# Mixture-of-experts weights in 8192-byte pieces, and expert slots scattered through memory, in a fused transformer layer

## The chip, the cores and the metric

The kernel runs on one core of a Trainium2 chip. The metric is the device time of one execution in microseconds (us). The profile is that of one execution by the hardware profiler; its engines are PE (TensorE matmul), PEld (TensorE weight load), DVE (VectorE), ACT (ScalarE), POOL (GpSimd) and SP (SyncE, which here only issues DMAs).

## The reference

One trunk layer of a generator over 512 latent tokens (and 256 context tokens) of width 2048. A first sub-layer mixes tokens with three recurrent heads groups; the change does not touch it. The second is a hierarchical mixture of experts over the 512 normalised tokens:

```python
grp = jnp.argmax(pg, -1)                      # 1 of 4 groups
top_p, top_i = lax.top_k(softmax(le), 2)      # 2 of its 8 experts
# every expert e (32 of them), on the tokens sent to it:
y = (silu(x @ w_gate[e]) * (x @ w_up[e])) @ w_down[e]   # 2048 -> 512 -> 2048
f = sum of a token's two y, weighted; out = rmsnorm(x + gt2 * f)
```

All is float32. The weights of the experts are 32 x 3 x 4 MB.

## The kernel before

The first 1890 us of the program (input projection, three recurrent mixers, output projection) stay as they are. Then come three stages.

**Routing** (`route_setup`, `route_tile`, `route_slots`). `route_slots` makes on DVE, for the tokens as 4 tiles of 128 rows, the one-hot rows `o1`, `o2` of the two chosen experts, the token's rank `pos` within each expert, and on POOL the weights `wm`. Each expert has 64 slots; `over` and `njob` count blocks of tokens beyond 64. `moe_over` is a hardware loop of `njob` rounds for those; all engines meet in front of it and behind it, and with no such block its body is skipped.

**Weights** (`moe_weights`, `load`, `slot`). SP streams all expert weights through a ring of 10 slots of 1 MB. `moe_weights` lists the chunks in the order of use: 8 gate/up chunks of an expert, 4 down chunks (half the columns of a pair of experts), and so on; `gf` is the last norm's gain. Four slots are there early (`more_slots(r0, NR)`), six after the output projection. A chunk of gate and up is 256 rows of each matrix, read by two DMAs of 512 KB, in which a partition gets two rows that lie together (4096 bytes); a down chunk is one DMA of 1 MB in pieces of 4096 bytes. Each `load()` waits until PE has used what was in the slot.

**Experts** (`phase_moe`). For each group of 4 experts `gather` makes a one-hot matrix `G` on DVE (`moe_hot`) and, for each of 8 slices of 256 rows, four products of 256 columns each with a high (`hh`, ACT) and a low part (`hl`, DVE, every fourth on POOL); the result `xg` is 256 slots wide. `gate_up(e)` multiplies `xg` with the ring: in each of 8 steps j there are 2 rows-of-128 times 2 halves `c` of columns, each product 64 slots by 512 columns (256 of gate beside 256 of up), the two halves in the two column halves of the array; a float32 product is two MATMUL instructions in the trace. It then loads the next chunk and calls the other work that is listed for step j. `turn` transposes, `down` multiplies with the down chunks, `combine` brings the slots back to the tokens with a one-hot `GT` and adds to `x1`. `slots(pr)` makes `GT` and the slots' weights `W` for a pair of experts, in three pieces: one-hot rows `Gp` on DVE, four PE transposes and an ACT copy, four PE products with `wm` and two DVE copies. PE's order in this stage is that of the code (`keep_in_program_order`).

Of the kernel before, what the change touches and what calls it, by code (L numbers as in the profile page):

```python
# [11 lines left out]
F32 = mybir.dt.float32  # L12
F32R = mybir.dt.float32r
BF = mybir.dt.bfloat16
# [38 lines left out]
class Kern:  # L53
# [1439 lines left out]
    def route_setup(self, op):  # L1493
# [27 lines left out]
        self.iota1k = rp.tile([P, 32], F32, name="iota1k")  # L1521
        nc.vector.tensor_scalar(self.iota1k, self.iota[:, :32], 1000.0, None, op0=OP.add)
        self.thr = rp.tile([P, 7], F32, name="thr")
        nc.vector.tensor_scalar(self.thr, self.iota[:, 1:8], 64.0, None, op0=OP.mult)
# [39 lines left out]
    def route_slots(self, tp):  # L1564
# [8 lines left out]

        def first_max(vals, n, oh, mx):
            t_ = mk(f"t{n}", n)
            ix = mk("ix", 1)
# [4 lines left out]
            nc.vector.tensor_tensor(oh, self.iota[:, None, :n].to_broadcast([P, 4, n]), bc(ix, n), op=OP.is_equal)  # L1581

        gm, og = mk("gm", 1), mk("og", 4)
        first_max(lgr, 4, og, gm)
        eg = mk("eg", 4)
# [12 lines left out]
        m1, m2, o1, o2 = mk("m1", 1), mk("m2", 1), mk("o1", 32), mk("o2", 32)  # L1598
        first_max(me, 32, o1, m1)
# [3 lines left out]
        first_max(me2, 32, o2, m2)  # L1603
        A = mk("A", 32)
# [31 lines left out]
        nc.gpsimd.tensor_tensor(me, o2, bc(e12[:, :, 1:2], 32), op=OP.mult)  # L1636
        nc.gpsimd.tensor_tensor(self.wm, self.wm, me, op=OP.add)

    def moe_hot(self, dst, es):
# [37 lines left out]
    def load(self):  # L1677
        nc, I = self.nc, self.I
        ch = next(self.todo, None)
        if ch is None:  # L1680
            return
        if ch == "gf":
            self.gf = self.slot([P, D], True)
            nc.sync.dma_start(self.gf, I["g_final"].rearrange("(o c) -> o c", o=1).to_broadcast([P, D]))
            return
        e, c = ch
        if type(c) is int:
            w = self.slot([P, 2, 2, 512])
            for j, nm in enumerate(("moe_w_gate", "moe_w_up")):
                nc.sync.dma_start(w[:, j], I[nm][0, e, 2 * c * P:(2 * c + 2) * P].rearrange("(p k) c -> p k c", k=2))  # L1690
        else:
            h, f = c
            w = self.slot([P, 2, D // 2])
            nc.sync.dma_start(w, I["moe_w_down"][0, e, 2 * f * P:(2 * f + 2) * P, h * D // 2:(h + 1) * D // 2].rearrange("(f p) c -> p f c", p=P))
        self.wgt[ch] = w

    def phase_moe(self):
        nc, tc = self.nc, self.tc
        wgt, load, NE = self.wgt, self.load, self.ne
        with tc.tile_pool(name="mo", bufs=1) as mo, tc.tile_pool(name="ps5", bufs=1, space=PSUM) as ps:  # L1700
# [9 lines left out]
            def gather(q):  # L1710
# [6 lines left out]
                for k0 in range(0, KT, 2):  # L1717
                    x = self.xgp.tile([P, 2, 256], F32, name=f"xg{k0 // 2}")
                    xg[q].append(x)
                    p = ps.tile([P, 2, 256], F32, name="pc_", bufs=4)  # L1720
                    for k in range(2):
                        h = self.h2[:, :, k0 * P + k:(k0 + 2) * P:2]
                        hh = mo.tile([P, 4, P], F32R, name="hh", bufs=2)
                        hl = mo.tile([P, 4, P], F32R, name="hl", bufs=2)
                        nc.scalar.copy(hh, h)  # L1725
                        (nc.gpsimd if k and k0 % 4 == 0 else nc.vector).tensor_tensor(hl, h, hh.bitcast(F32), op=OP.subtract)  # L1726
                        for i, hx in enumerate((hh, hl)):
                            for t in range(4):
                                mm(p[:, k], hx[:, t], G[:, t].rearrange("p e s -> p (e s)"), start=(i == t == 0), stop=(i == 1 and t == 3))
                    nc.scalar.copy(x, p)  # L1730
                    yield

            def slots(pr):

                es = (2 * pr, 2 * pr + 1)
                GT = mo.tile([P, S], F32R, name="GT", bufs=2)
                W = mo.tile([P, 1], F32, name="Wsl", bufs=2)
                Gp = mo.tile([P, 4, 2, 64], F32, name="Gp", bufs=1)
                self.moe_hot(Gp, es)
                yield  # L1740
                p = ps.tile([P, 4, P], F32, name="ts", bufs=1)
                for t in range(4):
                    tr(p[:, t], Gp[:, t].rearrange("p e s -> p (e s)"), self.ident)
                nc.scalar.copy(GT, p.rearrange("p t c -> p (t c)"))
                yield
                pw = ps.tile([P, 2], F32, name="ts", bufs=1)
                for t in range(4):
                    mm(pw, Gp[:, t].rearrange("p e s -> p (e s)"), self.wm[:, t, es[0]:es[0] + 2], start=(t == 0), stop=(t == 3))
                for i in range(2):
                    nc.vector.tensor_copy(W[64 * i:64 * i + 64], pw[64 * i:64 * i + 64, i:i + 1])  # L1750
                gts[pr] = (GT, W)
                yield

            def gate_up(e, *work):
# [3 lines left out]
                for j in range(KT // 2):  # L1758
                    g = wgt[e, j]
                    for k in range(2):  # L1760
                        for c in range(2):
                            mm(p[64 * c:64 * c + 64], x[j][:, k, 64 * (e % 4):64 * (e % 4) + 64], g[:, :, k, 256 * c:256 * c + 256],
                               start=(j == k == 0), stop=(j == 7 and k == 1), tile_position=(0, 64 * c))
                    load()
# [51 lines left out]
            for pr in range(NE // 2):  # L1816
                a = 2 * pr
                sl = slots(pr)
                if pr == 0:
# [4 lines left out]
                else:  # L1824
                    two = () if pr % 2 else ((0, partial(next, gat)),) * 2 + ((4, partial(next, gat)),) * 2
                    gate_up(a, *two, (1, partial(turn, a - 1)), (2, combine), (5, combine))
# [21 lines left out]
    def fin(self, mo, t, col):  # L1848
# [5 lines left out]
        sf = self.sf[:, t]  # L1854
        sq = mo.tile([P, col[1]], BF, name="sq3", tag="Gp", bufs=1)
        nc.scalar.activation(sq, x[:, cs], AF.Square, accum_out=sf[:, b:b + 1])
# [186 lines left out]
    def tail(self, ctx):  # L2043
# [22 lines left out]
        with ExitStack() as s:  # L2066
# [4 lines left out]
            next(r)  # L2071
            fin()
            next(r, None)
        self.moe_over()
# [83 lines left out]
```

## Time and profile before

| what | us |
|---|---|
| three runs: lowest, median, highest | 2979.39, 2993.38, 2997.74 |
| the profiled execution, its own time | 2985.22 |
| its span in the trace | 2983.5 |

The span is from the first to the last instruction of the trace. In the sections below, a row of a timeline has start (us from the span's start), length (us), engine, line and operation, output <- inputs, shape and count, and in brackets the idle time before it and what ended it. Matmuls overlap, so the pace of PE is read from one start to the next, not from a length.

### The profile page before, as it was taken

To read this page: it belongs to the slowest core of one execution; us is meant where nothing else is said; L and a number is where in the kernel's file an instruction comes from. 1 tells how busy PE (TensorE), PEld (TensorE's weight loads), DVE (VectorE), ACT (ScalarE), POOL (GpSimd) and SP (SyncE) were. 2 spreads that over 40 slices of the span, in tenths; PEclk is the share of its full clock that TensorE was granted. 3 is DMA by queue.
4 is the path that set the end of the run, shared out by engine and by line. 5 is a ranking of instruction groups with operands and counts; after the bars stand their busy time and mean duration, and the time that the engine had idled before them with its cause. 6 is when DMAs were issued, how large, how long until landed. Compare 5 with 4: busy or idle time off the path is not lost. (4 is left out here: it accounts for less than half of the span.)

```text
span 2983.5 us, 50569 instructions
## 1 busy us (share of the span) xinstructions
PE 2730.6 (92%) x19229; PEld 1798.6 (60%) x19229; DVE 1563.5 (52%) x3165; ACT 839.5 (28%) x1632; POOL 751.2 (25%) x715
## 2 busy tenths in 40 slices
PE   5989999988999999988989898879999999999997
PEld 3477787778767766766766666744454444544433
DVE  4366566688477565565446656642343333433335
ACT  4132322345432223322222322332121221211212
POOL 2332222231344443343344434520000000000001
PEclk9999999998999999999979989989999999999999
DMA  8858787887744344444465321469999999999997
GB/s 303 294 171 242 225 253 231 246 251 224 194 108 117 96 121 101 106 116 104 104 212 181 110 87 43 135 237 409 408 409 409 408 409 408 407 409 407 409 408 290
DMA packets 530909, 730.80 MB, mean 245 GB/s; under 512 B 121233, under 2 KB 347839, under 8 KB 529507
## 3 DMA queue, kind: packets, MB, share of 16 engines
q1 hardware_dynamic: 366864, 640.77, 59.9%
q10 hardware_dynamic: 161927, 81.17, 10.7%
q0 software_dynamic: 1872, 5.57, 0.6%
q8 instruction: 155, 2.54, 0.4%
q14 instruction: 91, 0.75, 0.1%
HBM read 672.50 MB, written 54.93 MB: 244 GB/s over the span
## 5 line engine op out<-in xcount | busy, mean ns | idle before, releaser
L1705 PE MATMUL pgu<-ring,xg 128*64 128x512 f32 x2048 | 484.4, 600 | 1.9 <-DVE sil__20834 L1770 0.9
L319 POOL TENSOR_TENSOR wl<-wr,wh 128x512 fp32r<-128x512 f32 x191 | 263.3, 1379 | 691.0 <-ACT wh L318 600.5
L61 PE MATMUL pl<-hil,wh 128*128 128x512 f32 x928 | 404.0, 436 | 4.3 <-ACT hil L253 3.7
L61 PE MATMUL pl<-lol,wh 128*128 128x512 f32 x928 | 376.4, 406 | 0.1
L61 PE MATMUL pl<-hil,wl 128*128 128x512 f32 x928 | 372.0, 401 | 0.5 <-POOL wl L319 0.4
L318 ACT CAST wh<-wr 128x512 fp32r<-128x512 f32 x292 | 179.6, 619 | 576.9 <-PE pl L61 316.7
L1705 PEld LDWEIGHTS pgu<-ring,xg 128*64 128x64 f32 x2048 | 135.1, 136 | 239.5 <-issue 225.3
L1726 POOL TENSOR_TENSOR hl<-h,hh 128x512 fp32r<-128x512 f32 x32 | 41.8, 1306 | 823.6 <-ACT hh L1725 823.6
L1705 PE MATMUL py<-ring,hT 128*64 128x512 f32 x1024 | 235.2, 593 | 3.5 <-DMA ring<-in_moe_w_down_dram 3.5
L271 DVE SCALAR_TENSOR_TENSOR acc<-w,sil,acc 128x512 f32<-128x512 f32 x240 | 197.6, 851 | 59.5 <-DMA w<-in_w_ada_dram 58.2
L61 PEld LDWEIGHTS pl<-hil,wh 128*128 128x128 f32 x928 | 178.8, 193 | 60.4 <-issue 14.4
L61 PEld LDWEIGHTS pl<-hil,wl 128*128 128x128 f32 x928 | 178.9, 193 | 41.2 <-POOL wl L319 1.2
L61 PEld LDWEIGHTS pl<-lol,wh 128*128 128x128 f32 x928 | 179.5, 193 | 38.5 <-issue 6.7
L1705 PEld LDWEIGHTS py<-ring,hT 128*64 128x64 f32 x1024 | 76.2, 137 | 155.8 <-issue 139.4
L61 PE MATMUL pc<-hic,wl 128*128 128x256 f32 x496 | 146.1, 295 | 14.4 <-DVE wl L319 10.5
L61 PE MATMUL pc<-hic,wh 128*128 128x256 f32 x496 | 146.3, 296 | 4.8 <-ACT wh L318 2.8
L61 PE MATMUL pc<-loc,wh 128*128 128x256 f32 x496 | 145.7, 295 | 1.1 <-DVE loc L254 1.1
L1725 ACT CAST hh<-h 128x512 fp32r<-128x512 f32 x128 | 84.8, 664 | 165.9 <-PE pc__23508 L1705 9.0
L1726 DVE TENSOR_TENSOR hl<-h,hh 128x512 fp32r<-128x512 f32 x96 | 66.6, 694 | 119.0 <-ACT hh L1725 114.8
L791 DVE TENSOR_TENSOR ptm<-Tm,Lay 64x1 f32<-64x1 f32 (+2 forms) x270 | 109.1, 404 | 22.3 <-DMA Lay<-s_ad 15.9
L1796 DVE SCALAR_TENSOR_TENSOR yt<-py,Wsl,g 128x512 f32<-128x512 f32 x64 | 48.1, 751 | 133.3 <-PE py L1705 133.3
L1443 POOL TENSOR_TENSOR wol<-wo,woh 128x512 fp32r<-128x512 f32 x56 | 75.3, 1347 | 159.7 <-PE acc L61 97.8
(2215 smaller groups left out, 4960.1 us busy)
## 6 DMA issues: line engine op xcount, KB each, us to landing
ring<-in_moe_w_gate_dram SPq DMA_DIRECT2D x256, 512.0 KB
ring<-in_moe_w_up_dram SPq DMA_DIRECT2D x256, 512.0 KB
ring<-in_moe_w_down_dram SPq DMA_DIRECT2D x128, 1024.0 KB
wr<-in_w_in_dram ACTq DMA_DIRECT2D x288, 256.0 KB
w<-in_w_ada_dram SPq DMA_DIRECT2D x256, 256.0 KB
w<-in_w_ada_dram SPq DMA_DIRECT2D x64, 512.0 KB
wo<-in_w_out_dram SPq DMA_DIRECT2D x56, 256.0 KB
rv_xk<-d_xk SPq DMA_DIRECT2D x36, 256.0 KB
```

The costliest lines, as they stand in the source:

```text
L61: i = self.nc.tensor.matmul(*a, **k)
L271: nc.vector.scalar_tensor_tensor(acc, w, self.sil[:, k, 0:1], acc, op0=OP.mult, op1=OP.add)
L318: nc.scalar.copy(wh[:, :, :n], wr[:, :, :n])
L319: (nc.vector if q in self.wdve else nc.gpsimd).tensor_tensor(wl[:, :, :n], wr[:, :, :n], wh[:, :, :n].bitcast(F32), op=OP.subtract)
L791: nc.vector.tensor_tensor(pt_[:, :t, :t], Tm[:, :t, :t], Lay[:, :t, t].rearrange("q (o s) -> q o s", o=1).to_broadcast([64, t, t]), op=OP. ...
L1443: nc.gpsimd.tensor_tensor(wl, w, wh.bitcast(F32), op=OP.subtract)
L1705: pin(nc.tensor.matmul(*a, **k))
L1725: nc.scalar.copy(hh, h)
L1726: (nc.gpsimd if k and k0 % 4 == 0 else nc.vector).tensor_tensor(hl, h, hh.bitcast(F32), op=OP.subtract)
L1796: nc.vector.scalar_tensor_tensor(yt, py, W, self.g2[:, col[0]:sum(col)], op0=OP.mult, op1=OP.mult)
```

## The change

Gate and up weights become chunks of their own: chunk c of an expert is 512 rows of gate (c even) or up (c odd), one DMA of 1 MB, in which a partition gets four rows that lie together (8192 bytes). A step j of `gate_up` takes 4 rows-of-128 of one matrix, in products of 256 columns. `slots` loses its PE work: after the ranks are known, eight indirect DMAs on POOL write (token, weight) pairs into a table in HBM at expert x 64 + rank, SP reads it back as `slot_tw`, and `GT` is one comparison on DVE. The gather pieces are called one to a step.

```diff
+        self.d_slot = self.scratch("d_slot", [16 * P + 2 * S, 2])
+        z = op.tile([P, 16, 2], F32, name="slot0")
+        nc.gpsimd.memset(z[:, :, 0], -1.0)
...
+        nc.sync.dma_start(self.d_slot[:16 * P].rearrange("(a p) c -> p a c", p=P), z)
...
         nc.gpsimd.tensor_tensor(self.wm, self.wm, me, op=OP.add)
+        yield
+
+        ad, fl, tw = mk("ad", 2), mk("fl", 2), mk("tw", 2, 2)
+        spare, sp_, in_ = mk("spare", 2), mk("sp", 32), mk("in", 2)
+        nc.gpsimd.iota(tw[:, :, :, 0], pattern=[[P, 4], [0, 2]], base=0, channel_multiplier=1, allow_small_or_imprecise_dtypes=True)
...
+        nc.gpsimd.tensor_copy(tw[:, :, :, 1], e12)
+        for i, (o, ix) in enumerate(((o1, ix1), (o2, ix2))):
+            nc.vector.tensor_tensor(sp_, self.pos, o, op=OP.mult)
+            red(ad[:, :, i], sp_, OP.add)
+            nc.vector.scalar_tensor_tensor(fl[:, :, i:i + 1], ix, 64.0, ad[:, :, i:i + 1], op0=OP.mult, op1=OP.add)
+        nc.vector.tensor_scalar(in_, ad, 64.0, None, op0=OP.is_lt)
+        nc.vector.tensor_tensor(fl, fl, spare, op=OP.subtract)
+        nc.vector.tensor_tensor(fl, fl, in_, op=OP.mult)
+        nc.vector.tensor_tensor(fl, fl, spare, op=OP.add)
+        at = tp.tile([P, 8], I32, name="at")
+        nc.vector.tensor_copy(at, fl.rearrange("p t i -> p (t i)"))
+        for i in range(8):
+            nc.gpsimd.indirect_dma_start(self.d_slot[:], bass.IndirectOffsetOnAxis(ap=at[:, i:i + 1], axis=0),
+                                         tw.rearrange("p t i c -> p (t i) c")[:, i], None)
+        self.slot_tw = rp.tile([P, 16, 2], F32, name="slot_tw")
+        nc.sync.dma_start(self.slot_tw, self.d_slot[:16 * P].rearrange("(a p) c -> p a c", p=P))
...
-            w = self.slot([P, 2, 2, 512])
-            for j, nm in enumerate(("moe_w_gate", "moe_w_up")):
-                nc.sync.dma_start(w[:, j], I[nm][0, e, 2 * c * P:(2 * c + 2) * P].rearrange("(p k) c -> p k c", k=2))
+            w = self.slot([P, 4, 512])
+            r = c // 2 * 512
+            nc.sync.dma_start(w, I[("moe_w_gate", "moe_w_up")[c % 2]][0, e, r:r + 512].rearrange("(p k) c -> p k c", k=4))
...
-                        h = self.h2[:, :, k0 * P + k:(k0 + 2) * P:2]
+                        h = self.h2[:, :, k0 // 4 * 512 + k0 % 4 + k:(k0 // 4 + 1) * 512:4]
...
+            nc.gpsimd.iota(tok, pattern=[[1, S]], base=0, channel_multiplier=0, allow_small_or_imprecise_dtypes=True)
             def slots(pr):
...
+                nc.vector.tensor_scalar(GT, tok, self.slot_tw[:, pr, 0:1], None, op0=OP.is_equal)
+                gts[pr] = (GT, self.slot_tw[:, pr, 1:2])
...
-                    for k in range(2):
+                    for k in range(4):
+                        kk = 4 * (j // 2) + k
                         for c in range(2):
-                            mm(p[64 * c:64 * c + 64], x[j][:, k, 64 * (e % 4):64 * (e % 4) + 64], g[:, :, k, 256 * c:256 * c + 256],
+                            mm(p[64 * c:64 * c + 64, j % 2], x[kk // 2][:, kk % 2, 64 * (e % 4):64 * (e % 4) + 64], w[:, k, 256 * c:256 * c + 256],
...
-                    two = () if pr % 2 else ((0, partial(next, gat)),) * 2 + ((4, partial(next, gat)),) * 2
+                    two = () if pr % 2 else tuple((j, partial(next, gat)) for j in (0, 1, 3, 4))
...
-                    two = ((3, partial(next, gat)),) * 2 + ((6, partial(next, gat)),) * 2
-                next(sl)
-                gate_up(a + 1, (0, partial(turn, a)), (1, combine), (2, partial(next, sl)), *two, (4, partial(next, sl)), (5, combine))
+                    two = tuple((j, partial(next, gat)) for j in (2, 3, 5, 6))
+                slots(pr)
+                gate_up(a + 1, (0, partial(turn, a)), (1, combine), *two, (5, combine))
```

POOL between the last of the routing and the loop of `moe_over` (`njob` is its count, `rt_wm` the weights, `h`/`hh`/`hl` the first gather), with what each waits for, before:

```order
L1637 TENSOR_TENSOR rt_wm<-rt_wm,rt_me 128x128 [waits Pool_49]
L1618 TENSOR_LOAD njob [waits DVE_49,PE_49,Activation_49]
L1877 COMPARE_AND_BRANCH
...
L1877 UNCONDITIONAL_BRANCH [waits barrier_Pool_Activation_PE_DVE_SP_gather]
...
L1726 TENSOR_TENSOR hl<-h_19443,hh 128x512 [waits Activation_49]
```

and now, where `d_slot` is the table, `at` its row numbers and DMASW the landings of POOL's own DMAs:

```order
L1643 TENSOR_TENSOR rt_wm<-rt_wm,rt_me 128x128 [waits Pool_49]
L1662 DMA d_slot<-rt_tw,at 3072x2 [waits DVE_49]
L1662 DMA d_slot<-rt_tw,at 3072x2 [waits DMASW5_49]
L1662 DMA d_slot<-rt_tw,at 3072x2 [waits DMASW6_49]
...
L1662 DMA d_slot<-rt_tw,at 3072x2 [waits DMASW3_49]
L1624 TENSOR_LOAD njob [waits DVE_49,PE_49,Activation_49]
L1893 COMPARE_AND_BRANCH
...
L1893 UNCONDITIONAL_BRANCH [waits barrier_Pool_Activation_PE_DVE_SP_gather]
...
L1762 IOTA tok 128x512
L1754 TENSOR_TENSOR hl<-h_19443,hh 128x512 [waits Activation_49]
```

Eight DMAs stand in front of the meeting of the engines, each behind the landing of the one before.

PE in the second expert of the second pair (`pgu` is gate and up, `ts` transposes and the slots' weights, `pc` gather and combine), before:

```order
L1705 MATMUL pgu<-ring_20873,xg_20532 64x512 x4
L1708 MATMUL ts<-ident,Gp 128x128 x4
L1705 MATMUL pgu<-ring_20880,xg_20567 64x512 x4
L1705 MATMUL pc__21007<-G,hh 128x256 x4
...
L1705 MATMUL pgu<-ring_20887,xg_20601 64x512 x4
L1705 MATMUL ts<-rt_wm,Gp 128x2 x4
L1705 MATMUL pgu<-ring_20894,xg_20635 64x512 x4
```

and now:

```order
L1733 MATMUL pgu<-ring_20951,xg_20560 64x256 x4
L1733 MATMUL pgu<-ring_20951,xg_20598 64x256 x4
L1733 MATMUL pc__21084<-G,hh 128x256 x4
...
L1733 MATMUL pgu<-ring_20961,xg_20560 64x256 x4
L1733 MATMUL pgu<-ring_20961,xg_20598 64x256 x4
L1733 MATMUL pc__21121<-G,hh 128x256 x4
...
L1733 MATMUL pgu<-ring_20971,xg_20635 64x256 x4
```

A step is twice as many products of half the columns, and the `ts` rows of `slots` are gone; those of `turn` stay.

## Rows read from the trace of the kernel before

**Rows 1.** The page: the span in 40 equal slices of 74.6 us, with the mean busy share of the 16 DMA engines in tenths, and the rate.

```profile
DMA  8858787887744344444465321469999999999997
GB/s 303 294 171 242 225 253 231 246 251 224 194 108 117 96 121 101 106 116 104 104 212 181 110 87 43 135 237 409 408 409 409 408 409 408 407 409 407 409 408 290
```

**Rows 2.** A window (us): its length, busy time of PE, PEld, DVE, ACT and POOL, then granted clock of PE, DMA share, GB/s.

```profile
1997.00:2953.00 956.00, 950.84 (x4644) 429.51 (x4640) 346.22 (x603) 171.64 (x315) 37.18 (x29) 1.00 1.02 407
```

**Rows 3.** The page's DMA issues of the ring.

```profile
ring<-in_moe_w_gate_dram SPq DMA_DIRECT2D x256, 512.0 KB
ring<-in_moe_w_up_dram SPq DMA_DIRECT2D x256, 512.0 KB
ring<-in_moe_w_down_dram SPq DMA_DIRECT2D x128, 1024.0 KB
```

**Rows 4.** The chain that ended last: start, length, what it was in. Two rows that are one period of four experts apart, and the last wait for a DMA.

```profile
2364.81 3.58 PE pgu L1705 x16
...
2488.29 3.58 PE pgu L1705 x16
...
2934.87 18.79 DMA ring<-in_moe_w_down_dram
```

**Rows 5.** Timeline of the experts: slots (`ts`), gate and up (`pgu`), combine (`pc`), down (`py`), turn (`ts` from `sil`), and a weight load beside gate and up.

```profile
2364.16 0.66 PE L1708 MATMUL ts<-ident,Gp 128*128 128x128 f32 x4
...
2364.74 3.65 PE L1705 MATMUL pgu<-ring,xg 128*64 128x512 f32 x16
...
2365.22 0.14 PEld L1705 LDWEIGHTS pgu<-ring,xg 128*64 128x64 f32 x2 [0.29 <-issue]
...
2368.33 1.05 PE L1705 MATMUL ts<-rt_wm,Gp 128*128 128x2 f32 x8
...
2369.31 1.94 PE L1705 MATMUL pgu<-ring,xg 128*64 128x512 f32 x8
...
2371.18 0.50 PE L1705 MATMUL pc__23135<-yeh,GT 128*128 128x512 f32 x1
...
2373.23 3.65 PE L1705 MATMUL pgu<-ring,xg 128*64 128x512 f32 x16
...
2376.72 7.04 PE L1705 MATMUL py<-ring,hT 128*64 128x512 f32 x32
...
2383.58 3.60 PE L1705 MATMUL pgu<-ring,xg 128*64 128x512 f32 x16
...
2387.12 0.44 PE L1708 MATMUL ts<-ident,sil__23165 128*128 128x128 f32 x2
...
2387.48 1.94 PE L1705 MATMUL pgu<-ring,xg 128*64 128x512 f32 x8
```

**Rows 6.** Timeline of PE alone: one step of a gather and the first products of the next.

```profile
2447.59 0.74 PE L1705 MATMUL pc__23619<-G,hh 128*128 128x256 f32 x4
2448.17 0.64 PE L1705 MATMUL pc__23619<-G,hl 128*128 128x256 f32 x4
2448.65 0.64 PE L1705 MATMUL pc__23619<-G,hh 128*128 128x256 f32 x4
...
2449.61 0.64 PE L1705 MATMUL pc__23646<-G,hh 128*128 128x256 f32 x4
```

**Rows 7.** Timeline of PE early in the program: float32 products of 256 columns with 32 rows of output, in the four column quarters of the array (`px`; once four of them, once eight), each group followed by another tile's product.

```profile
74.47 0.63 PE L61 MATMUL px<-w,sil 128*32 128x256 f32 x6
75.04 0.39 PE L61 MATMUL pc<-loc,wh 128*128 128x256 f32 x1
...
83.72 1.06 PE L61 MATMUL px<-w,sil 128*32 128x256 f32 x12
84.71 0.50 PE L61 MATMUL pl<-lol,wh 128*128 128x512 f32 x1
```

**Rows 8.** An issue on SP's queue, and windows as in rows 2 in which pieces of 8192 bytes land: token rows (`xt`) in the first, a vector (`g`) spread over the partitions in the second.

```profile
26.90 3.22 SPq L201 DMA_DIRECT2D xt<-in_x_dram  x2
...
32.00:34.00 2.00, 0.00 (x0) 0.00 (x0) 2.00 (x2) 1.80 (x2) 1.24 (x1) 1.00 1.02 421
...
1909.00:1911.00 2.00, 2.00 (x18) 1.91 (x18) 0.00 (x0) 1.38 (x4) 1.78 (x2) 1.00 1.06 430
```

**Rows 9.** Timeline of DVE: two small operations of the routing, then the last of the ranks and the first gather.

```profile
1952.74 0.16 DVE L1596 TENSOR_SCALAR rt_pen<-rt_og 128x16 f32<-128x16 f32 x1
...
1953.59 0.29 DVE L1578 TENSOR_TENSOR rt_t<-rt_me,rt_m 128x128 f32<-128x128 f32 x1
...
1959.97 0.13 DVE L1617 CAST njob<-nj 1x1 int32<-1x1 f32 x1
1963.12 1.43 DVE L1644 TENSOR_TENSOR G<-iota,rt_pos 128x256 fp32r<-128x256 f32 x4 [3.02 <-issue]
```

**Rows 10.** POOL's DMAs: KB each, and median us from issue to landing.

```profile
gl_la<-d_la POOLq DMA_DIRECT2D x8, 384.0 KB, 5.1
...
ltb<-in_k_lt_dram POOLq DMA_DIRECT2D x1, 64.0 KB, 3.3
```

**Rows 11.** SP's issues behind the loop, and in the first two steps of the first expert.

```profile
1965.59 0.34 SPq L1690 DMA_DIRECT2D ring<-in_moe_w_up_dram  x1
...
1977.32 0.33 SPq L1690 DMA_DIRECT2D ring<-in_moe_w_gate_dram  x1
...
1981.29 0.33 SPq L1690 DMA_DIRECT2D ring<-in_moe_w_gate_dram  x1
```

More of the change, by code (lines that the diff above doesn't have):

```diff
@@ L1522, in route_setup @@
         nc.vector.tensor_scalar(self.iota1k, self.iota[:, :32], 1000.0, None, op0=OP.add)
+        self.d_slot = self.scratch("d_slot", [16 * P + 2 * S, 2])
+        z = op.tile([P, 16, 2], F32, name="slot0")
+        nc.gpsimd.memset(z[:, :, 0], -1.0)
+        nc.gpsimd.memset(z[:, :, 1], 0.0)
+        nc.sync.dma_start(self.d_slot[:16 * P].rearrange("(a p) c -> p a c", p=P), z)
         self.thr = rp.tile([P, 7], F32, name="thr")
@@ L1572, in route_slots, with first_max @@
         lgr, lex = L[:, :, :4], L[:, :, 4:]
-        def first_max(vals, n, oh, mx):
+        def first_max(vals, n, oh, mx, id_):
             t_ = mk(f"t{n}", n)
-            ix = mk("ix", 1)
+            ix = mk(f"ix{id_}", 1)
             red(mx[:, :, 0], vals, OP.max)
@@ L1581, in first_max @@
             nc.vector.tensor_tensor(oh, self.iota[:, None, :n].to_broadcast([P, 4, n]), bc(ix, n), op=OP.is_equal)
+            return ix
         gm, og = mk("gm", 1), mk("og", 4)
-        first_max(lgr, 4, og, gm)
+        first_max(lgr, 4, og, gm, 0)
         eg = mk("eg", 4)
@@ L1598, in route_slots @@
         m1, m2, o1, o2 = mk("m1", 1), mk("m2", 1), mk("o1", 32), mk("o2", 32)
-        first_max(me, 32, o1, m1)
+        ix1 = first_max(me, 32, o1, m1, 1)
         me2 = mk("me2", 32)
@@ L1602, in route_slots @@
         nc.vector.tensor_scalar(me2, me2, -3e38, None, op0=OP.max)
-        first_max(me2, 32, o2, m2)
+        ix2 = first_max(me2, 32, o2, m2, 2)
         A = mk("A", 32)
@@ L1637, in route_slots @@
         nc.gpsimd.tensor_tensor(self.wm, self.wm, me, op=OP.add)
+        yield
+        ad, fl, tw = mk("ad", 2), mk("fl", 2), mk("tw", 2, 2)
+        spare, sp_, in_ = mk("spare", 2), mk("sp", 32), mk("in", 2)
+        nc.gpsimd.iota(tw[:, :, :, 0], pattern=[[P, 4], [0, 2]], base=0, channel_multiplier=1, allow_small_or_imprecise_dtypes=True)
+        nc.gpsimd.iota(spare, pattern=[[P, 4], [S, 2]], base=16 * P, channel_multiplier=1, allow_small_or_imprecise_dtypes=True)
+        nc.gpsimd.tensor_copy(tw[:, :, :, 1], e12)
[14 more added lines that the diff above has]
+        nc.sync.dma_start(self.slot_tw, self.d_slot[:16 * P].rearrange("(a p) c -> p a c", p=P))
     def moe_hot(self, dst, es):
@@ L1731, in gather @@
                     yield
+            tok = mo.tile([P, S], F32, name="tok")
+            nc.gpsimd.iota(tok, pattern=[[1, S]], base=0, channel_multiplier=0, allow_small_or_imprecise_dtypes=True)
             def slots(pr):
-                es = (2 * pr, 2 * pr + 1)
                 GT = mo.tile([P, S], F32R, name="GT", bufs=2)
[L1737 to L1752, printed above, removed]
+                nc.vector.tensor_scalar(GT, tok, self.slot_tw[:, pr, 0:1], None, op0=OP.is_equal)
+                gts[pr] = (GT, self.slot_tw[:, pr, 1:2])
             def gate_up(e, *work):
@@ L1758, in gate_up @@
                 for j in range(KT // 2):
-                    g = wgt[e, j]
-                    for k in range(2):
+                    w = wgt[e, j]
+                    for k in range(4):
+                        kk = 4 * (j // 2) + k
                         for c in range(2):
-                            mm(p[64 * c:64 * c + 64], x[j][:, k, 64 * (e % 4):64 * (e % 4) + 64], g[:, :, k, 256 * c:256 * c + 256],
-                               start=(j == k == 0), stop=(j == 7 and k == 1), tile_position=(0, 64 * c))
+                            mm(p[64 * c:64 * c + 64, j % 2], x[kk // 2][:, kk % 2, 64 * (e % 4):64 * (e % 4) + 64], w[:, k, 256 * c:256 * c + 256],
+                               start=(j == k == 0), stop=(j == 7 and k == 3), tile_position=(0, 64 * c))
                     load()
@@ L1817, in phase_moe @@
                 a = 2 * pr
-                sl = slots(pr)
                 if pr == 0:
@@ L1854, in fin @@
         sf = self.sf[:, t]
-        sq = mo.tile([P, col[1]], BF, name="sq3", tag="Gp", bufs=1)
+        sq = mo.tile([P, col[1]], BF, name="sq3", tag="hl", bufs=2)
         nc.scalar.activation(sq, x[:, cs], AF.Square, accum_out=sf[:, b:b + 1])
@@ L2072, in tail @@
             fin()
+            next(r)
             next(r, None)
```

## Prediction

> **What bounds the kernel now.** I read the 40 slices first, then the experts' stretch as one window, then the chain that ended last, and last the timeline of PE. The slices show 407 to 409 GB/s and full DMA engines from the 28th slice on, nowhere before [rows 1]. In the window from 1997 to 2953 us the DMA share is 1.02 at 407 GB/s, and PE counts 951 of 956 us as busy, but at overlapping lengths [rows 2]. The ring brings 256 x 2 x 512 KB of gate and up and 128 x 1024 KB of down [rows 3], 402.7 MB, 12.58 MB an expert. In the chain the same place of the code returns after 2488.29 - 2364.81 = 123.48 us [rows 4]; four experts are 50.33 MB, and 50.33 MB in 123.48 us are 407.6 GB/s. So the stage runs at the rate of the DMA engines, and the chain's last wait is for a down chunk [rows 4].
>
> PE's own need for four experts, from start to start [rows 5, 6]: gate and up 16 instructions in 2376.72 - 2373.23 = 3.49 us, a tenth or so of that the change-over; inside a run a pair of column halves takes 0.14 + 0.29 = 0.43 us, and 4 x 32 pairs are 55.0 us. Down 2383.58 - 2376.72 = 6.86 us for half the columns of a pair of experts, four times, 27.4. Combine 2373.23 - 2371.18 = 2.05, eight times, 16.4. Gather 2449.61 - 2447.59 = 2.02, eight times, 16.2. Turn 0.36, four times, 1.4. Slots 0.58 (2364.16 to 2364.74) and 0.98 (2368.33 to 2369.31), twice, 3.1. Together 119.5 us of 123.5: PE would be the next bound, 4.0 us (3%) behind.
>
> **Gate and up in pieces of 8192 bytes.** The routing holds 10 slots (10.5 MB) when the experts start, so 268.4 - 10.5 = 257.9 MB of gate and up remain. At 408 GB/s they take 632.1 us. Of a stream in 8192-byte pieces the trace has short pieces only: 421 GB/s over 2 us of token rows, at the same share of 1.02, and 430 over 2 us of the spread vector, at a share of 1.06 [rows 8]. I take 421, because its share is that of the experts' window: 612.6 us, a gain of 19.5. Bounds: 408, nothing; 430, 599.8 us, a gain of 32.3. Four experts would then take 33.55 MB at 421 (79.7) and 16.78 MB at 408 (41.1), 120.8 us.
>
> **Products of 256 columns, and no slots on PE.** PE loses the 3.1 us of slots: 116.4. It keeps as many columns, in twice as many products. Four float32 products of 256 columns in the four quarters of the array take 75.04 - 74.47 = 0.57 us with the change-over, eight take 84.71 - 83.72 = 0.99; the second four cost 0.42 [rows 7], which is no more than the 0.43 of as many columns in one pair now. The two weight loads of a pair take 0.14 of 0.43 us now [rows 5] and would take 0.14 of 0.215. So I count nothing, and PE needs some 116.4 against 120.8: it stays behind the DMA. What hides the halving is the load of the next weights beside the running product; if that cover is gone, see the second rival. The upper bound, from the gather's products of 256 columns: four in 0.48 us [rows 6], 0.12 each; against the 0.107 that half of a pair of 0.43 us gives, 0.013 more for each of 4 x 128 instructions, 6.7 us, and PE would be at 123.1.
>
> **The scatter.** Here the start of the experts waits. In front of the loop of `moe_over` POOL now has eight indirect DMAs, each of which waits for the landing of the last, and all engines meet behind them; the gather on DVE, the products on PE and SP's loads are queued behind that meeting. Now the count is there at 1959.97 + 0.13 = 1960.10, and the first gather starts 3.02 us later [rows 9]. DVE gets eleven operations first: four of 128x128 at 0.29 us and seven small ones at 0.16 [rows 9], 2.3 us. Then eight landings. The trace has no scatter; POOL's smallest DMA took 3.3 us from issue to landing (64 KB), its next 5.1 (384 KB) [rows 10]. A scatter of 128 pairs of 8 bytes is nearest to the first, so 8 x 3.3 = 26.4 us. From below: 64 KB at 407 GB/s are 0.2 us, so 8 x 3.1 = 24.8, unless the waits between them are free, and then one landing, 3.3; from above 8 x 5.1 = 40.8. Of the 3.02 us of the loop I leave 2, since part of it passes while the last scatter lands. The first gather starts at 1960.1 + 2.3 + 26.4 + 2 = 1990.8 instead of 1963.1: 27.7 us late.
>
> Nothing hides this. The ring is full by then: SP's next loads start when a step of gate and up frees a slot, at 1977.32 and 4.0 us later at 1981.29 [rows 11]. SP now gets all ten chunks out ahead of the loop, where it had the last 2.5 MB behind it (from 1965.59 [rows 11]); these had landed before 1977 anyway, so nothing comes back. The read of the table stands in SP's queue behind the loop, ahead of a load that waits for PE, and its consumer `slots` runs an expert later: nothing. On POOL the 512-wide iota is ahead of the first `hl`; under 1 us, between nothing and 1, I take 0.5. The comparison for `GT` takes the place of `Gp`, a copy on ACT and two on DVE, engines that have 346 and 172 of 956 us of work [rows 2]: nothing. The gather pieces move by a step or two inside PE's list; PE is not the bound: nothing.
>
> The Trainium skill (page "DMA: Bandwidth & Descriptors", section "Anatomy of one DMA — SWDGE (gpsimd) path") puts the fixed cost of a DMA issued from GpSimd at about 2.0 us. No row here is that short; the shortest is the 3.3 us of rows 10. By the page the eight would take an estimated 16 us and the time would be 10.4 us less.
>
> **Sum**, on the profiled execution: 2985.2 (span 2983.5 and 1.7 around it) + 27.7 + 0.5 - 19.5 = 2993.9. That execution is 8.2 us below the median of the three runs, 2993.4, which spread over 18 us; carried to the median it is 3002. I put the number between the two, at 2998: a gain in the stage that the start gives back.
>
> **Rivals**, on the profiled execution's scale, as differences.
> 1. The scatter is cheap. If POOL does not wait for each landing, or they land faster than any DMA of POOL's here, one landing and eight issues remain, some 6 us in place of 26.4, and with the higher rate (430) the sum is +2.3 + 6 + 2 - 3 - 32.3 = -25. Against it: the order shows a wait at each, on the last one's landing. With only one of the two, about -5 to -12.
> 2. PE becomes the bound, and it is slower: the weight loads of 64 columns are not hidden by 215 ns of product. If the two loads of a pair go one behind the other, 0.28 us a pair, gate and up of four experts take 4 x 64 x 0.28 = 71.7 instead of 55.0, PE needs 133.1, and 7.75 such periods (390 MB of 50.33) are 7.75 x 9.6 = 74 us longer than now; with the scatter +102. It decides from the point where a pair costs over 0.215 + 4.4/256 = 0.232 us. For it: twice as many loads in the same time. Against it: rows 7, where four loads stand beside the same 0.21 us of product.
> 3. Pieces of 8192 bytes are no faster in a long stream, because something other than the cost of a piece sets 408 GB/s: then the gain is nothing and the scatter stays, +28. The short windows speak against it, but they are 2 us long. Beside this mechanism: the Trainium skill (same page, section "Where 436 GB/s comes from") has HBM bind a core's loads at about 358 GB/s, by which piece length would not matter; the trace, at 407 for 956 us, does not agree with the number.
> 4. The scatters are dear, 5.1 us each: +42 + 0.5 - 19.5 = +23. At 7 us each, +38.
>
> **How the numbers follow.** Three runs of the kernel before spread by 0.6%, so about 1%, 30 us, can be told from no change. My forecast has 0.55, the first rival 0.13 (0.05 of it below -30), the second 0.07, the third 0.13, the fourth 0.12. Slower by over 1% are the second, a third of the third, half of the fourth (scatters over 6 us), and some 0.03 of the forecast's own spread: 0.20. Faster by over 1%: 0.06. The range reaches from the first rival, 2998 - 25, to the third and fourth, 2998 + 32: 2973 to 3030; the second stays out.
>
> **What would show it.** Right: in the experts' windows 415 to 425 GB/s as a mean over gate, up and down, a period of four experts of 120 to 121.5 us, PE with small gaps; between the last of the ranks and the first gather about 30 us with DMA idle and eight DMAs on POOL, 3.3 us apart. Wrong: a rate of 408 (third rival); a rate that falls below 407 with slots full and PE's pairs 0.24 us or more apart (second); scatters under 2 us apart (first) or over 5 (fourth).

## The result, and the profile after

The changed kernel takes 3021.47 us (median of 4 runs, 3016.72 to 3028.80) against 2986.39 us (4 runs, 2978.47 to 2997.74) for the kernel before: a ratio of 1.0116, 95% interval 1.0088 to 1.0143, 35 us slower. The range held it; the number was 23 us too low, and the sign of the experts' term was wrong. In the two profiled executions the 37.7 us lie here (the cast is that of [rows 9]):

| stretch, us | before | after | difference | forecast |
|---|---|---|---|---|
| start to the end of the cast of `njob` | 1960.1 | 1967.9 | +7.8 | 0 |
| from there to the first `G` | 3.0 | 27.0 | +24.0 | +27.7 |
| first `G` to the end of the span | 1020.4 | 1026.3 | +5.9 | -19.5 and +0.5 |

The page of the changed kernel, DMA share and rate in 40 slices of 75.5 us, to be read against [rows 1]:

```profile
DMA  8858788887644344444474322449999999999996
GB/s 298 293 174 235 226 246 247 240 247 226 188 105 104 96 117 110 107 110 102 109 240 142 102 90 54 163 149 416 410 410 412 395 415 402 391 415 398 416 398 277
```

The flat 407 to 409 of before has become 391 to 416: the longer pieces do run faster, but not all the time. Before the experts, the 27th slice has 149 GB/s, since a stretch without loads lies in it. DVE's and POOL's timelines of that stretch (start, length, operation, in brackets the wait before it and what ended it), which answer to [rows 9]:

```profile
1967.76 0.13 DVE L1623 CAST njob<-nj 1x1 int32<-1x1 f32 x1
...
1970.05 0.17 DVE L1660 CAST at<-rt_fl 128x8 int32<-128x8 f32 x1
1994.91 1.43 DVE L1672 TENSOR_TENSOR G<-iota,rt_pos 128x256 fp32r<-128x256 f32 x4 [24.69 <-issue]
```

```profile
1970.52 1.15 POOL L1662 DMA_INDIRECT d_slot<-rt_tw,at  x1 [3.62 <-DVE at L1660]
1977.12 0.97 POOL L1662 DMA_INDIRECT d_slot<-rt_tw,at  x1 [5.45 <-DMA d_slot<-rt_tw,at]
1979.50 0.96 POOL L1662 DMA_INDIRECT d_slot<-rt_tw,at  x1 [1.41 <-DMA d_slot<-rt_tw,at]
...
1991.46 0.96 POOL L1662 DMA_INDIRECT d_slot<-rt_tw,at  x1 [1.41 <-DMA d_slot<-rt_tw,at]
```

Each scatter waits for the one before, as forecast: 6.6 us to the second, then 2.4 us a step, and all engines start behind the last. The first is long because the last ring loads, issued at 1968.85 and 1969.23, still land: from 1972 to 1974 us the DMA engines move 418 GB/s, from 1978 on next to nothing.

In the experts' stretch a period of four experts takes 124.4 us (mean of four periods, from `G` to `G`) against 123.4 before, where 120.8 was forecast. A little more than one period of the changed kernel in windows (start and end, length, busy time of PE, PEld, DVE, ACT and POOL, granted clock, DMA share, GB/s):

```profile
2505.00:2515.00 10.00, 10.00 (x62) 4.28 (x60) 3.31 (x5) 1.87 (x4) 0.00 (x0) 1.00 0.93 362
2515.00:2525.00 10.00, 10.00 (x81) 6.37 (x76) 2.48 (x4) 0.00 (x0) 0.00 (x0) 1.00 0.99 383
2525.00:2545.00 20.00, 20.00 (x132) 10.68 (x132) 7.12 (x12) 1.99 (x4) 0.00 (x0) 1.00 1.02 421
2545.00:2568.00 23.00, 20.97 (x125) 10.14 (x125) 5.88 (x10) 1.00 (x2) 0.00 (x0) 0.93 1.02 415
2568.00:2595.00 27.00, 27.00 (x203) 19.09 (x201) 12.84 (x16) 11.43 (x14) 1.64 (x2) 1.00 1.02 417
2595.00:2615.00 20.00, 20.00 (x136) 11.70 (x133) 8.20 (x11) 7.54 (x11) 2.98 (x2) 1.00 1.00 400
2615.00:2640.00 25.00, 25.00 (x178) 14.75 (x176) 12.92 (x19) 7.37 (x10) 1.75 (x1) 1.00 0.96 360
```

PE and the DMA take turns at waiting. Toward the end of the two experts with gathers and just behind them the rate sinks to 360: PE is the slower there, and SP, whose loads wait for what PE has used, has no free slot. In the two without, the DMA runs at 415 to 421, and from 2545 to 2568 PE counts 20.97 of 23 us as busy. The chain that ended last (start, length) shows on what, the answer to the last line of [rows 4]:

```profile
2517.70 7.06 PE pgu L1733 x64
...
2526.80 3.60 PE pgu L1733 x32
2530.40 6.87 PE py L1733 x32
2537.27 3.45 PE pgu L1733 x32
...
2541.05 20.14 DMA ring<-in_moe_w_down_dram
...
2561.23 6.41 PE py L1733 x21
...
2570.37 1.88 PE pgu L1733 x16
```

A down chunk issued at 2541.05 lands 20.14 us later, behind the loads that were issued ahead of it, and the next product of the down waits for it; the same wait of 20 to 22 us stands once in each period of the chain. Counted from start to start of PE's instructions, four experts of the changed kernel take 58.76 us of gate and up, 16.46 of combine, 16.66 of gather, 1.41 of turn and 31.05 of down, of which 3.56 are this wait: a need of 120.8 us. The kernel before, counted in the same way, has 58.54, 16.35, 16.11, 1.47, 27.66 and 3.14 of slots: 123.3 of its 123.4.

### The profile page after: what moved, and what is told of

It is laid out like the page before. It is cut to its first block, busy times and chain, and to the rows that moved or that the text cites. A ratio compares the mean times of both kernels' runs of the same rounds, so it can differ in the third digit from the quotient of the medians.

```text
span 3021.2 us, 53744 instructions
## 1 busy us (share of the span) xinstructions
PE 2732.1 (90%) x21085; PEld 1936.5 (64%) x21085; DVE 1590.0 (53%) x3096; ACT 889.2 (29%) x1616; POOL 771.3 (26%) x729
## 5 line engine op out<-in xcount | busy, mean ns | idle before, releaser
L1733 PE MATMUL pgu<-ring,xg 128*64 128x256 f32 x4096 | 484.4, 383 | 1.9 <-DVE sil__20803 L1787 0.9
L1733 PEld LDWEIGHTS pgu<-ring,xg 128*64 128x64 f32 x4096 | 285.6, 137 | 173.6 <-issue 38.4
L1733 PE MATMUL py<-ring,hT 128*64 128x512 f32 x1024 | 247.8, 608 | 18.1 <-DMA ring<-in_moe_w_down_dram 18.1
L1754 POOL TENSOR_TENSOR hl<-h,hh 128x512 fp32r<-128x512 f32 x32 | 53.1, 1659 | 814.2 <-ACT hh L1753 814.2
L1753 ACT CAST hh<-h 128x512 fp32r<-128x512 f32 x128 | 140.7, 1146 | 164.6 <-PE pc__21084 L1733 6.1
L1754 DVE TENSOR_TENSOR hl<-h,hh 128x512 fp32r<-128x512 f32 x96 | 104.7, 1110 | 140.8 <-ACT hh L1753 140.8
L1813 DVE SCALAR_TENSOR_TENSOR yt<-py,slot_tw,g 128x512 f32<-128x512 f32 x64 | 48.0, 750 | 160.6 <-PE py L1733 160.6
```

Source lines behind the costliest of these rows:

```text
L1733: pin(nc.tensor.matmul(*a, **k))
L1813: nc.vector.scalar_tensor_tensor(yt, py, W, self.g2[:, col[0]:sum(col)], op0=OP.mult, op1=OP.mult)
```

## The experiments

Theory after the result: PE (120.8) and the DMA (some 121) now need the same time, and the ring is too shallow for the swing between experts with and without a gather. Rivals: the pieces or the single gathers themselves slow the stage; the DMA does not hold a higher rate; and, for the start, the scatters are given back later wherever they stand. "G to end" is from the first `G` to the end of the span, "period" as above; both are of the profiled executions. Where an expectation counts the stage to the last down (982, 1003), that is some 23 us less than "G to end"; the 1001 to 1026 of the pieces alone and the scatters alone are "G to end".

| run | median us | ratio to before, 95% | cast to G | G to end | period |
|---|---|---|---|---|---|
| before | 2986 to 2988 | | 3.0 | 1020.4 | 123.4 |
| changed | 3021.5 | 1.0116 (1.0088, 1.0143) | 27.0 | 1026.3 | 124.4 |
| pieces alone | 3014.7 | 1.0096 (1.0066, 1.0126) | 3.0 | 1051.3 | 127.5 |
| the same, rows two apart | 2992.4 | 1.0020 (1.0003, 1.0037) | 3.0 | 1020.5 | 123.5 |
| scatters alone | 3011.9 | 1.0086 (1.0058, 1.0114) | 27.2 | 1018.8 | 123.4 |
| changed, paired gathers | 3029.0 | 1.0135 (1.0099, 1.0171) | 27.8 | 1033.2 | 125.1 |
| changed, without `yel` | 3003.8 | 1.0067 (1.0042, 1.0092) | 26.7 | 1009.5 | 122.4 |
| changed, downs in halves | 3001.7 | 1.0055 (1.0035, 1.0076) | 26.6 | 1006.3 | 121.8 |
| changed, scatters behind the loop | 3003.9 | 1.0068 (1.0036, 1.0099) | 7.2 | 1029.5 | 124.0 |
| the two remedies | 2983.6 | 0.9983 (0.9964, 1.0002) | 7.2 | 1005.0 | 121.6 |
| before, table initialised | 2988.9 | 1.0008 (0.9988, 1.0027) | 3.0 | 1020.3 | 123.4 |
| remedies, all eight behind | 2970.5 | 0.9936 (0.9912, 0.9960) | 5.1 | 1004.6 | 121.5 |

**The pieces alone.** The kernel before with the change's `load`, `gate_up` and the gather's rows four apart:

```
-            w = self.slot([P, 2, 2, 512])
+            w = self.slot([P, 4, 512])
...
-                        h = self.h2[:, :, k0 * P + k:(k0 + 2) * P:2]
+                        h = self.h2[:, :, k0 // 4 * 512 + k0 % 4 + k:(k0 // 4 + 1) * 512:4]
```

> The kernel before with only the loads and products of the experts' gate and up changed (apart, 8192-byte pieces, 256-column products); slots and gathers stay. Theory: the stage was already held by PE, whose work for four experts took 123.0 us of the 123.48, so faster pieces have nothing to give: stage 1020 us (G's first row to its last down) +-6, total within 6 us of the kernel before, 2980 to 2995. Rival A (the pieces bring what the forecast gave them, 421 against 408 GB/s): stage about 1001, total about 2967. Rival B (the pieces themselves slow the stage, because the rate is not held or the ring of 1 MB slots now stalls): stage 1026 or more, total 2992 or more, and PE waits for ring chunks with several us a period.

28 us slower, so the theory fails and the size is that of rival B, but not for its reason: PE waits less for down chunks (0.6 us a period) than in the changed kernel; its gathers take 19.2 us instead of 16.1. The chain shows on what, at one of these gathers:

```profile
2345.27 1.14 ACT hh L1725
...
2346.43 1.09 DVE hl L1726
...
2347.57 1.78 PE pc__23244 L1705 x12
```

The second of two gather steps waits for the copies. Grouped by form (count, busy us and mean ns of one behind the bar, then the idle time before), first in the kernel before, then in the changed kernel, each from 2100 to 2600 us:

```profile
L1725 ACT CAST hh<-h 128x512 fp32r<-128x512 f32 x64 | 42.5, 665 | 85.4 <-PE pc__23508 L1705 9.0 <-PE pc__24309 L1705 9.0 <-PE pc__22707 L1705 9.0
...
L1726 DVE TENSOR_TENSOR hl<-h,hh 128x512 fp32r<-128x512 f32 x48 | 33.2, 692 | 56.8 <-ACT hh L1725 56.7
```

```profile
L1753 ACT CAST hh<-h 128x512 fp32r<-128x512 f32 x64 | 70.2, 1146 | 90.1 <-PE pc__21945 L1733 6.1 <-PE pc__24528 L1733 6.1 <-PE pc__22806 L1733 6.1
L1754 DVE TENSOR_TENSOR hl<-h,hh 128x512 fp32r<-128x512 f32 x48 | 52.2, 1109 | 73.2 <-ACT hh L1753 73.2
```

As many elements, read 16 bytes apart instead of 8, take 1.15 us instead of 0.67 on ACT and 1.11 instead of 0.69 on DVE. The Trainium skill (page "SBUF — State Buffer", section "Specifications (TRN2)") gives the memory lines of 16 bytes and wants two hits in a line for full speed: 8 bytes apart makes two hits, 16 makes one, and these rows agree.

**The same with rows two apart**, which pairs rows and weights wrongly:

```
-                        h = self.h2[:, :, k0 // 4 * 512 + k0 % 4 + k:(k0 // 4 + 1) * 512:4]
+                        h = self.h2[:, :, k0 * P + k:(k0 + 2) * P:2]
```

> As the run with the pieces alone (gate and up apart, 256-column products, paired gathers, old slots; 3015 us, period of four experts 127.5), but the gather reads its rows two apart, as in the kernel before, instead of four apart, so that rows and weights pair up wrongly. Theory: the copies hh (ACT 1.13 us against 0.66) and hl (DVE 1.10 against 0.69) that read 16 bytes apart make the paired gather wait: with 8 bytes apart PE's time for the gathers of a period returns from 19.2 to 16.1 us, the period to 124 to 124.5, total 2986 to 2994. Rival (the pieces or the single 1 MB loads themselves stall the ring): gather 16.1, but the time goes to waits for ring chunks, period 126.5 or more, total 3007 or more.

The theory holds: gathers back at 16.1 us, period at 123.5, 22 of the 28 us gone in the medians and 31 in "G to end". In the chain the gather's two steps now stand one behind the other:

```profile
2334.46 2.11 PE pc__23217 L1705 x16
2336.57 1.92 PE pc__23244 L1705 x16
```

It also shows that the pieces and the 256-column products by themselves bring nothing and cost next to nothing as long as PE has the slots: PE needs 123.5 us of this period, "G to end" is 0.1 us off, and the ratio's interval leaves 1 to 11 us over the whole time.

**The scatters alone.** The changed kernel with `load`, `gate_up`, the gather's rows and its paired steps as before, so that only the table, `slots` and the scatters differ.

> The kernel before with only the slots' tokens and weights scattered and read back (pieces of 4096 bytes, 512-column products and the paired gathers stay). Theory: +24 us between the njob cast and the first G, up to +5 before it, and PE loses 3.1 us of slots in each period; if the DMA then bounds the stage at 408 GB/s it stays at 1018 to 1021, total 3008 to 3020. Rival (408 GB/s in the kernel before was PE's pace and not the DMA's limit): the stage falls by up to 3.1 x 7.75 = 24 us, total 2986 to 2996, and the rate in the saturated stretches rises above 412.

The theory holds: 24.2 us more between cast and `G`. PE has lost its 3.1 us of slots, and the period stays at 123.4: its downs take 31.2 us of a period instead of 27.7, since they wait for chunks, at this rate (the page's 40 slices, the experts from the 28th on):

```profile
GB/s 298 297 174 233 223 252 237 241 256 221 196 109 106 94 120 117 102 110 101 111 246 139 103 91 54 149 157 409 409 409 409 409 409 406 409 409 408 409 408 285
```

So 408 to 409 (one slice has 406) is the limit of the pieces of 4096 bytes, also with slack on PE. In the kernel before both limits stood at 123.4 us.

**The changed kernel with paired gathers:**

```
-                    two = () if pr % 2 else tuple((j, partial(next, gat)) for j in (0, 1, 3, 4))
+                    two = () if pr % 2 else ((0, partial(next, gat)),) * 2 + ((4, partial(next, gat)),) * 2
...
-                    two = tuple((j, partial(next, gat)) for j in (2, 3, 5, 6))
+                    two = ((3, partial(next, gat)),) * 2 + ((6, partial(next, gat)),) * 2
```

> The changed kernel with the gathers' steps two at a time, as they stood in the kernel before. Theory (PE at 120.8 and DMA at 120.8 in balance with a ring too shallow to carry the swing between experts with and without a gather): four fewer change-overs of 0.25 to 0.35 us a period give 1.0 to 1.4 us, 8 to 11 us at most, and half of it is likely lost in the ring: total 3010 to 3021. Rival (the single steps are what slows the stage): the period falls from 125.3 to 122 or less, total 2995 or less. Other rival (two steps together make the swing larger): slower than the changed kernel by 3 to 10 us.

Slower by 7.5 us in the medians, whose intervals overlap, and by 6.9 behind the first `G` in the profiles: the size of the other rival, which I had put down to a larger swing. PE's gathers take 19.2 us again. The single steps are no burden: they give ACT and DVE time for the slower copies (16.7 us).

**Without the products of `yel`** (the low part of the experts' results, the second of combine's two products):

```
-                    for j, y in enumerate((yh, yl)):
-                        mm(p, gts[pr][0][:, t * P:(t + 1) * P], y, start=(j == 0), stop=(j == 1))
+                    for y in (yh,):
+                        mm(p, gts[pr][0][:, t * P:(t + 1) * P], y, start=True, stop=True)
```

> The changed kernel without the products of yel in combine, 8.2 us of PE's work in a period, so that PE has slack and the DMA alone sets the period of 50.33 MB. If pieces of 8192 bytes are moved at 421 GB/s and the downs' 4096 at 408, the period is 120.8 us against 124.4 in the changed kernel, total 2992 to 2997. Rival (the rate is not held in this stage, 404 to 408 with slack as well): period 123.4 to 124.4, total 3013 or more.

Between the two. The products were worth 6.6 us of a period and not 8.2; PE is idle for 5 to 6 us of it, and the windows of this run hold

```profile
2125.90:2249.00 123.10, 117.33 (x816) 67.63 (x814) 49.42 (x71) 29.29 (x40) 6.39 (x4) 1.00 1.02 417
2374.00:2498.10 124.10, 119.23 (x816) 67.97 (x814) 50.15 (x71) 29.34 (x41) 6.37 (x4) 0.99 1.01 411
```

411 to 417 GB/s: at 417 the 50.33 MB of a period take 120.7 us. So the forecast's mean of 416.6 was the right size for the DMA, and even with slack on PE the ring loses 1 to 2 us of it.

**Downs that give back two slots at a time.** In the changed kernel a down of two blocks of columns keeps its four chunks until its end. Here it takes the chunks of f 0 and 1 for both blocks, gives these back, then takes the others:

```
+                for g in range(2):
+                    for col in cols:
+                        for f in (2 * g, 2 * g + 1):
...
+                    load()
+                    load()
```

> The changed kernel, in which a down of two column blocks first takes the two chunks of f 0 and 1 for both blocks, gives their slots back, and then the other two; PE's work is the same. Theory (PE at 120.8 and DMA at 120.8 would both fit, but the ring of 10 slots, of which a down holds four at once, cannot carry the swing): PE's 3.6 us of waiting for down chunks in a period fall to 1 or less, period 121.5 to 122.5, total 2997 to 3010. Rival (the DMA's own rate is the limit, 404 to 408): the wait moves to another place, total within 4 us of the changed kernel.

Confirmed: 20 us less than the changed kernel, period 121.8, with PE's work unchanged; its downs take 28.5 us of a period instead of 31.1. Of 6.6 periods, waits of PE and its weight loads for down chunks (sum, times, longest), first the changed kernel, then this run:

```profile
PEld py L1733 <- DMA ring<-in_moe_w_down_dram: 22.4, 12, 2.8
PE py L1733 <- DMA ring<-in_moe_w_down_dram: 13.0, 13, 1.9
```

```profile
PEld py L1733 <- DMA ring<-in_moe_w_down_dram: 11.2, 9, 1.9
PE py L1733 <- DMA ring<-in_moe_w_down_dram: 4.4, 6, 1.0
```

The rate in the page's slices is now 411 to 417 from the 29th to the 39th:

```profile
GB/s 301 295 173 235 225 254 242 242 251 226 193 102 107 97 120 99 103 117 100 103 229 167 111 92 38 128 143 404 416 416 415 413 417 411 415 416 414 416 413 288
```

The change also makes one DMA of 1 MB out of two of 512 KB. That is not what raises the rate: a down chunk always was one DMA of 1 MB. Two windows of this run, the first with pieces of 8192 bytes alone, the second with downs alone:

```profile
2431.00:2437.00 6.00, 6.00 (x42) 3.14 (x40) 2.89 (x4) 1.61 (x3) 0.00 (x0) 1.00 1.02 422
2510.00:2516.00 6.00, 6.00 (x56) 3.84 (x53) 0.00 (x0) 0.00 (x0) 0.00 (x0) 1.00 1.02 406
```

**The scatters behind the loop.** Seven of eight issue beside the first gather; its low parts are all on DVE; `slots(pr - 1)` is called ahead of its down:

```
+                    self.scatter()
...
+                    slots(pr - 1)
                     for col in COLS[:2]:
```

> The changed kernel with seven of the eight scatters and the read of the slots' table moved behind the loop, beside the first gather; GT is made one pair later. Theory: the 24 us between the njob cast and G fall to 3 to 5, and nothing of the stage waits for the table, total 2995 to 3002. Rival (the chain is given back later: the scatters' packets or DVE's wait for the table hold the first gather): gain below 12 us, total 3009 or more, and a wait for slot_tw of 5 us or more stands in DVE's rows.

17.5 us less than the changed kernel, where the theory had 19 to 26: part of the rival is true. DVE reaches `GT` in the middle of the first gather and waits for the table there:

```profile
1994.17 0.88 DVE L1772 TENSOR_SCALAR GT<-tok,slot_tw 128x512 fp32r<-128x512 f32 x2 [10.60 <-DMA slot_tw<-d_slot]
```

The first gather takes 40.3 us from its `G` to the next `G`, 8.0 more than in the changed kernel.

**Both remedies**, with `GT` ordered behind the first gather's low parts on DVE:

> The two remedies together: scatters behind the loop with GT ordered behind the first gather's low parts, so that DVE's 10.6 us of waiting for the slots' table in the first gather goes, and the downs that give back two slots at a time. Theory: scatters behind the loop -24, downs -8 to -24, total 2970 to 2990, at or under the kernel before. Rival (the first gather stays 8 us longer whatever DVE's order, since the scatters' packets stand beside the ring's): stage from G at least 1003, total 2995 or more.

The theory holds. The first gather takes 31.7 us, so it was DVE's order and not the scatters' packets. The time is that of the kernel before.

**The table's initialising alone**, in the kernel before:

> The kernel before with only the initialising of the slots' table added: two memsets and one DMA of 2048 pieces of 8 bytes on SP, ahead of the first ring loads; nothing reads it. Theory (the njob cast came 7.8 us later in the changed kernel's trace by the drift between executions): total within 3 us of the kernel before. Rival (the small packets delay the loads behind them): 4 to 8 us slower.

The medians cannot decide: 0.8 us apart, by the ratio's interval -4 to +8. Nor can the cast of `njob`, which ends here at 1955.2 us, earlier than in the kernel before: by then executions have drifted apart by ten us and more (1951.5 to 1973.5 us in the kernels that initialise the table in 8-byte pieces, 1955.1 to 1960.1 in the three that have no table). A shorter stretch decides. SP issues the initialising just behind its last store of `d_y`, ahead of the last weights of the output projection (`w`), inside what I had called the unchanged first 1890 us. From that store's issue to the end of the cast it is 82.8 to 83.4 us in the three kernels without a table and 86.4 to 89.7 in the eight with 8-byte pieces, 87.5 in this run, where nothing else was changed: 4.6 us between the means. So in this stretch the rival is right. The initialising holds up the issue of a small DMA on ACT's queue (`br`; 1.1 to 1.2 us in the four kernels without 8-byte pieces, 3.0 to 4.7 in the eight with them); behind it stand the loads of `w`, and DVE waits for those. The kernel before, the changed kernel and this run:

```profile
1881.48 1.15 ACTq L1499 DMA_DIRECT2D br__19459<-in_moe_b_rg_dram  x1
...
1888.53 1.31 DVE L1479 TENSOR_TENSOR w<-w,gt 128x512 f32<-128x512 f32 x2 [3.68 <-DMA w<-in_w_out_dram]
```

```profile
1885.02 4.23 ACTq L1499 DMA_DIRECT2D br__19459<-in_moe_b_rg_dram  x1
...
1895.12 1.29 DVE L1479 TENSOR_TENSOR w<-w,gt 128x512 f32<-128x512 f32 x2 [6.26 <-DMA w<-in_w_out_dram]
```

```profile
1872.67 3.68 ACTq L1499 DMA_DIRECT2D br__19459<-in_moe_b_rg_dram  x1
...
1882.84 1.29 DVE L1479 TENSOR_TENSOR w<-w,gt 128x512 f32<-128x512 f32 x2 [6.94 <-DMA w<-in_w_out_dram]
```

The DMA engines, from 1 us behind the issue of the initialising (1871.03) in this run, were full and moved 29 GB/s:

```profile
1872.00:1876.00 4.00, 3.81 (x18) 2.84 (x17) 3.17 (x5) 0.62 (x1) 1.28 (x1) 1.00 1.32 29
```

**Both remedies, all eight scatters behind the loop**, and the table initialised in pieces of 128 bytes:

```
-        nc.sync.dma_start(self.d_slot[:16 * P].rearrange("(a p) c -> p a c", p=P), z)
+        nc.sync.dma_start(self.d_slot[:16 * P].rearrange("(p a) c -> p a c", p=P), z)
...
+            self.tc.keep_in_program_order(d)
```

> The two remedies together, and all eight scatters behind the loop (the run before had one ahead of it: 7.2 us from the njob cast to G), and the table initialised in 128 pieces of 128 bytes. Theory: stage 982 us as with the two remedies, 16 less than in the kernel before, and 3 to 4 us from the njob cast to G: total 2968 to 2978, faster than both kernels. Rival (the part ahead of the loop stays late, or the eighth scatter holds the first gather): total 2980 to 2990.

Faster than both kernels, 17.6 us under the one before. From the last store of `d_y` to the cast it takes 82.7 us, as without a table, so the 8-byte pieces were the cost of the initialising. DVE's and POOL's timelines:

```profile
1957.02 0.13 DVE L1623 CAST njob<-nj 1x1 int32<-1x1 f32 x1
...
1962.26 1.43 DVE L1678 TENSOR_TENSOR G<-iota,rt_pos 128x256 fp32r<-128x256 f32 x4 [2.78 <-issue]
```

```profile
1961.45 1.15 POOL L1667 DMA_INDIRECT d_slot<-rt_tw,at  x1 [0.20 <-issue]
1965.11 1.39 POOL L1667 DMA_INDIRECT d_slot<-rt_tw,at  x1 [2.51 <-DMA d_slot<-rt_tw,at]
1971.07 0.96 POOL L1667 DMA_INDIRECT d_slot<-rt_tw,at  x1 [4.57 <-DMA d_slot<-rt_tw,at]
...
1994.08 1.24 POOL L1671 DMA_DIRECT2D slot_tw<-d_slot  x1 [3.40 <-DMA d_slot<-rt_tw,at]
```

What is left of the start is DVE's eleven operations: 5.1 us from cast to `G`, 2.1 more than before. The chain of scatters takes 32.6 us here instead of 24, but beside the first gather nobody waits for it.

## Why the prediction was right and wrong

- **The range held by luck.** It reached to the third and fourth rivals, whose mechanisms did not come; the forecast's own -19.5 came out as +5.9, and a cost that the sum left out came on top.
- **The scatter** (+27.7): right in mechanism and nearly in size, +24.0. DVE's part took 2.3 us as counted; the eight landings took 24.0 (1970.52 to the next operation behind the loop, 1994.5) instead of 26.4, as one of 6.6, beside the last ring loads, and seven at 2.4 to 3. By the Trainium skill's 2.0 us for a DMA from GpSimd (page "DMA: Bandwidth & Descriptors", section "Anatomy of one DMA — SWDGE (gpsimd) path") the eight were an estimated 16; the measured step is 2.4 where the DMA engines were idle, a fifth over the figure. The first rival (cheap scatters) and the fourth (dear ones) both fall.
- **The pieces of 8192 bytes** (-19.5): the rate was right, 415 to 421 in the windows where the DMA is the bound and 411 to 417 with slack on PE; the third rival's mechanism (no faster in a long stream) falls, though its +28 came nearer to the profiles' +37.7 than the forecast's +8.7 did, and the fourth's +38, for scatters of 7 us each that did not come, hit it. The gain did not arrive: +5.9.
- **The step that failed** is "PE needs some 116.4 against 120.8: it stays behind the DMA". PE's need was 120.8. The mis-sized term is gate and up, 55.0 for what takes 58.5: I took the time of a pair inside a run and 3.49 for a run with its start, and let the starts of the runs go. The chain has runs of 16, 32 and 64 instructions at 1.88, 3.60 and 7.06 us: 0.108 for one and some 0.15 for the start of a run, of which a period has about two dozen; a run right behind a down starts without it (16 at 1.73 us). The gathers add 0.5. [rows 2] had PE busy in 951 of 956 us; I explained that away with overlapping lengths.
- **What followed from it.** With PE and the DMA both at 121 the ring must carry the swing between the experts, and a down that holds four of ten slots until its end does not let it. That is shown: the same work with slots given back two at a time is at 121.8.
- **256-column products at no cost**: right. 32 of them take 3.60 us, 16 of 512 columns took 3.58 [rows 4]; the second rival's mechanism falls.
- **The moved gathers, "nothing"**: right in sum, for a reason that I had not seen. The rows four apart make the copies 0.4 to 0.5 us longer; with paired steps that costs some 7 us in the changed kernel, and 22 by the medians where PE has the slots as well; the single steps hide it.
- **Left out: the table's initialising.** The sum has nothing ahead of the cast. The 2048 pieces of 8 bytes cost some 4.6 us there, by the stretch from the last store of `d_y` to the cast in all the profiles, and nothing when they were 128 pieces of 128 bytes. With 24.0 and 5.9 that makes 34.5 of the 35.1 us between the medians. The rest of the +7.8 in the first pair of profiles is drift from before that store.
- **Open.** Executions drift by ten us and more ahead of the cast, so the terms can be added up to the medians only within that. A deeper ring was not tried.

## What to carry to other kernels

Before a faster transfer is counted as a gain, add up the next engine's need from start to start over a whole period, starts of runs included: an engine at 99.5% busy is a second bound, not a spare. Where two bounds meet, how buffers are given back decides how much of either reaches the end, and halving what a consumer holds can be worth more than the faster transfer. A serial chain of small DMAs belongs beside work that does not need it, with its consumer placed late in its engine's queue. A DMA of many small pieces belongs where no load is waited for, or in longer pieces, even if nothing reads it soon.

## What the runs showed of the hardware

- A float32 read 16 bytes apart instead of 8 took 1.15 us against 0.67 on ACT and 1.11 against 0.69 on DVE for 128x512.
- Indirect scatters of 128 pieces of 8 bytes, one behind the other: 2.4 us a step with idle DMA engines; beside the ring's loads 6.6 (the first in the changed kernel) and 2.4 to 6.0 (the last run).
- A store of 2048 pieces of 8 bytes (16 KB) held the DMA engines at a share of 1.32 and 29 GB/s for 4 us, and an issue on another engine's queue took 3.0 to 4.7 us instead of 1.1 to 1.2; stored in 128 pieces of 128 bytes the same table delayed nothing.
- A long stream in pieces of 4096 bytes stood at 406 to 409 GB/s, whether or not PE had slack; with two thirds of it in pieces of 8192 it reached 411 to 421. In windows of 6 us with one kind alone it was 406 and 422.
